# The up projection of a hybrid block as one sequence of 77 products, with weight splits three products ahead and the convolution in pieces

## The chip, the cores and the metric

The kernel runs on one core of a Trainium2 chip. The metric is the device time of one execution in microseconds (us), shown as the median of three runs. The core's engines are TensorE (PE in the profile; its weight loads PEld), VectorE (DVE), ScalarE (ACT), GpSimd (POOL) and SyncE (SP), and 16 DMA engines that all queues share. GpSimd and SP issue the transfers here: SP plain loads, GpSimd the transfers that add to their target.

## The reference

One transformer block on 512 tokens of width 1024: a recurrent mixer, a cross attention and a feed-forward network, each followed by a scaled residual and a layer norm. The change touches the feed-forward part:

```python
def conv_ffn(x, w_up, conv_w, conv_b, w_down):
    u = causal_dwconv(x @ w_up, conv_w, conv_b)
    gate, val = jnp.split(u, 2, axis=-1)
    return (jax.nn.gelu(gate) * val) @ w_down

x = layer_norm(ALPHA * x + ca, ln2_g[l], ln2_b[l])
ff = conv_ffn(x, ffn_w_up[l], ffn_conv_w[l], ffn_conv_b[l], ffn_w_down[l])
x = layer_norm(ALPHA * x + ff, ln3_g[l], ln3_b[l])
```

`w_up` is 1024 x 5632 in float32, the convolution has three taps along the tokens, `w_down` is 2816 x 1024.

## The kernel before

Every float32 product is made of three matmuls: each operand is split into a high part (cast to fp32r by ScalarE: `wh` for weights, line 125) and the rest (subtracted by VectorE: `wl`, line 126), and `mm3` (lines 155 to 157) adds high x high, and the two mixed terms. A split thus is a cast on ScalarE and then a subtraction on VectorE, for 128 x 1024 weights at a time; `wh` and `wl` have four buffers each.

The up projection saves work by Winograd's form of Strassen's scheme. Its weights lie in HBM as 11 column groups ("quads", q = 0 to 10), each of four blocks B11, B12, B21, B22 of 512 KB. Seven products replace eight. They are called here by the names that the changed kernel gives them, with the weights they use: M1 (B11), M2 (B21), M3 (B22), M7 (B22+B12), M6 (B11+B22+B12), M5 (T1 = B11+B12), M4 (B21+B11+B22+B12); M7.2 is that of quad 2. The left operands are sums of blocks of the activations (`xf` tiles, made by `forms_block`, lines 794 to 817, from four 128-token blocks after LN2: A11, A12 from blocks 0 and 1; S1 to S4 and A22 from blocks 2 and 3). One product is 24 matmuls of 256 columns. The sums of weights are made by transfers: `add` in `up_forms` (line 848) is a GpSimd transfer that adds HBM or SBUF data to an SBUF slot. In a quad the order is load B11, B21, B22; after the split of B22, B22 += B12; T1 = B11 loaded, += B12; B11 += the sum; B21 += that. Seven slots of 512 KB (`rawx` and the halves of the three `raw` tiles) hold the blocks in turn.

`quad` (line 870) writes, from quad 2 on, M3, M1, M2, M7, M6, M5, M4, with a split just ahead of each product, ScalarE's copies of partial results (line 880), VectorE's adds into `uu` (line 884), and then the whole convolution of the quad: for two halves and two `j`, ScalarE's first tap (`fc`, line 918), two taps on VectorE (line 920), GELU (line 922) and the product (line 923). For quads 0 and 1 M1 and M2 come first; M1.0 and M2.0 stand before the last transposes of the LN2 result (`x2_last`, line 927). The text sets no order here: the tile scheduler places the instructions on each engine by its own costs, and each engine then runs its list in order. The last slab ahead of this part multiplies by `ca_wo` (line 824); its block results go through `ln2_evict` (residual, statistics, norm; a small reciprocal-root op of each block runs on GpSimd, line 428). After it comes the down projection: `slab` over 22 `k` in units of two, each unit a split of `w_down` and of the hidden activations (`h_split`, line 939).

Of the kernel before, what the change touches and what calls it, by code (L numbers as in the profile page):

```python
# [40 lines left out]
def hybrid_block_kernel(  # L41
# [777 lines left out]
    def ln2_evict(b, ps):  # L819
        resid(b, ps, 512, 1024)  # L820
        norm(b)
        return lambda: forms_block(b)
# [16 lines left out]
    blocks = [q2.tile([P, 1024], F32, name="rawx")]  # L839
    for _ in range(3):  # L840
        r = wp.tile([P, 2048], F32, name="raw", tag="raw", bufs=3)
        blocks += [r[:, 0:1024], r[:, 1024:2048]]

    def up_forms(q, order):
        blk = lambda kh, ch: ffn_w_up[q, kh, ch]
        at = {n: blocks[(4 * q + i) % 7] for i, n in enumerate(order + ("T1",))}
        r1, r2, r3, r4 = (at[n] for n in ("B11", "B22", "B21", "T1"))
        load, add = nc.sync.dma_start, lambda d, s_: nc.gpsimd.dma_start(d, s_, accum_op=OP.add)
        src = {"B11": blk(0, 0), "B22": blk(1, 1), "B21": blk(1, 0)}
        for n in order:  # L850
            load(at[n], src[n])
        for n in order:
            yield split(at[n], (8, P), 16)
            if n == "B22":
                add(r2, blk(0, 1))
        load(r4, blk(0, 0))
        add(r4, blk(0, 1))
        add(r1, r2)
        add(r3, r1)
        for r in (r2, r1, r4, r3):  # L860
            yield split(r, (8, P), 16)
# [8 lines left out]
    def quad(q):  # L870

        early = q < 2
        us = up_forms(q, ("B11", "B21", "B22") if early else ("B22", "B11", "B21"))
        uu = (hf[3 + q] if early else raws[q % 2]).rearrange("p (c j t) -> p c j t", c=2, j=2)
        g2 = lambda t: t.rearrange("p (j t) -> p j t", j=2)
        t1, t2_ = slice(0, 256), slice(256, 512)

        def kept(bank, name):
            t = t2(name)
            A.copy(t, bank)  # L880
            return g2(t)

        def put(dst, bank, other):
            V.tensor_tensor(dst, g2(bank), other, op=OP.add)

        def third():
            b = mx_bank()
            product(b, "S4", next(us), True, True)
            return kept(b, "m3")

        if not early:
            m3 = third()
        bp = mm_bank()
        product(bp, "A11", next(us), True, False)
        m1 = kept(bp, "m1")
        b = mx_bank()
        product(b, "A12", next(us), True, True)
        put(uu[:, 0, :, t1], b, m1)
        if early:
            yield  # L900
            m3 = third()
        b4 = mm_bank()
        product(b4, "S3", next(us), True, False)
        m7 = kept(b4, "m7")
        product(bp, "S2", next(us), False, False)
        u2 = kept(bp, "u2")
        product(bp, "S1", next(us), False, True)
        put(uu[:, 1, :, t1], bp, m3)
        put(uu[:, 1, :, t2_], bp, m7)
        product(b4, "A22", next(us), False, True)  # L910
        put(uu[:, 0, :, t2_], b4, u2)
        for c in (1, 0):
            y = []
            for j in range(2):
                ft = j * NPAIR + 2 * q + c
                u, f = uu[:, c, j, :], t2("fc")
                w = lambda i: ncols[:, i * 44 + ft:i * 44 + ft + 1] if c else col(FCW + i * 44 + ft)
                A.activation(f, u, AF.Identity, bias=col(FCB + ft), scale=w(2))  # L918
                for d in (1, 2):
                    V.scalar_tensor_tensor(f[:, d:], u[:, :S - d], w(2 - d), f[:, d:], op0=OP.mult, op1=OP.add)  # L920
                y.append(f)
            A.activation(y[0], y[0], AF.Gelu_apprx_tanh)
            V.tensor_mul(hslice(2 * q + c), y[0], y[1])

    early = [quad(q) for q in range(2)]
    next(early[0])
    x2_last()
    next(early[1])
    for g in early:
        for _ in g:  # L930
# [72 lines left out]
```

## Time and profile before

| what | value |
|---|---|
| median of 3 runs | 874.77 us (873.73 to 875.7) |
| profiled execution, device time | 872.24 us |
| span of its profile | 870.5 us |
| PE busy | 806.2 us (93%) |
| DVE busy | 570.4 us (66%) |
| ACT busy | 376.3 us (43%) |
| DMA queue of the loads (q1), share of 16 engines | 33.4% |
| DMA queue of the adding transfers (q0) | 14.3% |

Times within the profile count from the span's start. "Idle before" in square brackets after an instruction is how long its engine stood before it, and what released it. The granted clock (PEclk) is that of TensorE, as a share of full speed. A matmul's own duration overlaps its neighbours', so a product's length is read from the starts of two neighbours.

### The profile page before, as it was taken

How to read it: one execution, taken by the hardware profiler on the slowest of the kernel's cores; microseconds unless marked ns; L12 is line 12 of the kernel's file. 1: busy time of each engine (PE TensorE's matmuls, PEld its weight loads, DVE VectorE, ACT ScalarE, POOL GpSimd, SP SyncE). 2: the span in 40 equal slices, each digit the busy share in tenths (PEclk: the TensorE clock that was granted, in tenths of full speed). 3: DMA queues.
4: the chain of work that ended last, by engine and by line, in shares of the span. 5: the costliest groups of instructions: out<-in, count | busy, mean ns of one | idle time of the engine just before them, and what ended most of it. 6: DMA issues, size and time to landing. Idle time of an engine off the chain costs nothing. (4 is left out here: it accounts for less than half of the span.)

```text
span 870.5 us, 11772 instructions
## 1 busy us (share of the span) xinstructions
PE 806.2 (93%) x4696; PEld 709.3 (81%) x4696; DVE 570.4 (66%) x944; ACT 376.3 (43%) x512; POOL 68.3 (8%) x96
## 2 busy tenths in 40 slices
PE   9979999999999999999995778888898788999996
PEld 7858877787798888889884778888898788888885
DVE  6463498898783893385596377776666768934227
ACT  2289543553252052273152355555544557721110
POOL 1000001001100000000000111101111110000001
PEclk9989999999999999999998788999989899999999
DMA  9936742353257142313401777677686866422202
GB/s 263 184 75 168 105 77 45 91 125 105 79 203 258 48 145 98 97 63 132 121 2 25 184 191 161 158 174 172 152 187 171 194 150 161 173 97 97 73 1 98
DMA packets 53183, 111.05 MB, mean 128 GB/s; under 512 B 3844, under 2 KB 21380, under 8 KB 53128
## 3 DMA queue, kind: packets, MB, share of 16 engines
q1 hardware_dynamic: 46208, 84.58, 33.4%
q0 software_dynamic: 6336, 23.07, 14.3%
q10 hardware_dynamic: 584, 2.64, 0.9%
q8 instruction: 37, 0.61, 0.3%
q14 instruction: 18, 0.15, 0.1%
HBM read 96.63 MB, written 2.12 MB: 113 GB/s over the span
## 5 line engine op out<-in xcount | busy, mean ns | idle before, releaser
L126 DVE TENSOR_TENSOR wl<-raw,wh 128x1024 fp32r<-128x1024 f32 x155 | 187.4, 1221 | 172.3 <-ACT wh L125 171.6
L125 ACT CAST wh<-raw 128x1024 fp32r<-128x1024 f32 x155 | 161.7, 1051 | 311.3 <-PE mm L157 126.2
L157 PE MATMUL mm<-xf,wl 128*128 128x256 f32 x440 | 133.0, 303 | 32.2 <-DVE wl L126 32.1
L155 PE MATMUL mm<-xf,wh 128*128 128x256 f32 x440 | 133.4, 304 | 8.9 <-ACT wh L125 8.1
L156 PE MATMUL mm<-xf,wh 128*128 128x256 f32 x440 | 131.0, 299 | 0.0
L157 PEld LDWEIGHTS mm<-xf,wl 128*128 128x128 f32 x440 | 93.0, 211 | 35.0 <-DVE wl L126 35.0
L155 PEld LDWEIGHTS mm<-xf,wh 128*128 128x128 f32 x440 | 93.1, 212 | 11.4 <-ACT wh L125 8.7
L156 PEld LDWEIGHTS mm<-xf,wh 128*128 128x128 f32 x440 | 92.9, 211 | 0.0
L156 PE MATMUL mm<-wl,hTh 128*128 128x512 f32 (+1 forms) x180 | 65.9, 366 | 0.0
L155 PE MATMUL mm<-wh,hTh 128*128 128x512 f32 (+1 forms) x180 | 65.8, 366 | 0.0
L157 PE MATMUL mm<-wh,hTl 128*128 128x512 f32 (+1 forms) x180 | 65.8, 365 | 0.0
L155 PE MATMUL mm<-wh,xTh 128*128 128x512 f32 x128 | 52.5, 410 | 0.4 <-DVE xTh L285 0.4
L156 PE MATMUL mm<-wl,xTh 128*128 128x512 f32 x128 | 52.0, 406 | 0.0
L157 PE MATMUL mm<-wh,xTl 128*128 128x512 f32 x128 | 51.5, 402 | 0.0
L155 PE MATMUL mm<-xTh,wh 128*128 128x512 f32 x128 | 51.2, 400 | 0.0
L157 PE MATMUL mx<-xf,wl 128*128 128x256 f32 x176 | 49.4, 280 | 1.9 <-DVE wl L126 1.9
L156 PE MATMUL mm<-xTl,wh 128*128 128x512 f32 x128 | 51.1, 399 | 0.0
L157 PE MATMUL mm<-xTh,wl 128*128 128x512 f32 x128 | 51.0, 398 | 0.0
L156 PE MATMUL mx<-xf,wh 128*128 128x256 f32 x176 | 49.5, 281 | 0.8 <-DVE xf L247 0.8
L155 PE MATMUL mx<-xf,wh 128*128 128x256 f32 x176 | 49.9, 284 | 0.2 <-ACT wh L125 0.2
L920 DVE SCALAR_TENSOR_TENSOR fc<-xfr,ncols,fc 128x511 f32<-128x511 f32 (+1 forms) x36 | 25.0, 748 | 24.1 <-ACT fc L918 24.1
L155 PEld LDWEIGHTS mm<-wh,hTh 128*128 128x128 f32 x180 | 34.0, 189 | 5.6
(312 smaller groups left out, 1764.0 us busy)
## 6 DMA issues: line engine op xcount, KB each, us to landing
raw<-in_ffn_w_up_dram SPq DMA_DIRECT2D x37, 512.0 KB, 4.5
raw<-in_w_in_dram SPq DMA_DIRECT2D x14, 1024.0 KB, 8.4
raw<-in_ffn_w_down_dram SPq DMA_DIRECT2D x10, 1024.0 KB, 5.1
raw<-in_ffn_w_up_dram POOLq DMA_DIRECT2D x19, 512.0 KB, 8.6
raw<-in_ca_wkv_dram SPq DMA_DIRECT2D x8, 1024.0 KB, 5.3
raw<-raw POOLq DMA_DIRECT2D x15, 512.0 KB, 4.7
raw<-in_w_out_dram SPq DMA_DIRECT2D x4, 1024.0 KB, 8.9
raw<-in_ca_wq_dram SPq DMA_DIRECT2D x4, 1024.0 KB, 5.0
```

What stands on the lines that cost most here:

```text
L125: A.copy(hv, src)
L126: V.tensor_sub(lv, src, f32(hv))
L155: T.matmul(ps, ah, bh, start=first, stop=False, skip_group_check=True)
L156: T.matmul(ps, ah, bl, start=False, stop=False, skip_group_check=True)
L157: T.matmul(ps, al, bh, start=False, stop=last, skip_group_check=True)
L920: V.scalar_tensor_tensor(f[:, d:], u[:, :S - d], w(2 - d), f[:, d:], op0=OP.mult, op1=OP.add)
```

## The change

The generator `quad` is replaced by `seq`, one list of 77 (product, quad) pairs, and `step(i)`, which writes for one product: the copies and adds that the product before left over (`posts`), the split of product i + 3, loads due then (`AHEAD`), the 24 matmuls, and one of five pieces of a finished quad's convolution. The list begins M1, M2 of quads 0, 1 and 2, goes on with a hand-made mix of quads 0 to 3, and from quad 3 on is M1, M2, M7, M6, M3 of the next quad, M5, M4. From step 6 on, the written order is kept on PE, ACT, DVE and GpSimd (`manual_schedule`); before that the scheduler places the instructions. There are nine slots (two halves of an `hf` tile are new), given out by `take` and `drop`. The first loads move into the `ca_wo` slab (`ffn_begin`), and quad 0 gets a second copy of B22, T3, to which B12 is added before M3.0. Splits for the first three units of the down projection are written in the last three steps.

```diff
-    def slab(xh, xl, w, c0, nk, evict, blocks=NB, late=0, mid=None, mid_k=4, halves=False, pre=None):
+    def slab(xh, xl, w, c0, nk, evict, blocks=NB, late=0, mid=None, mid_k=4, halves=False, units=None):
...
-    x2_last = slab(tok(oTh), tok(oTl), ca_wo[0], 512, KT, ln2_evict, late=4)
...
+    def ffn_begin():
+        half = lambda t: [t[:, 0:1024], t[:, 1024:2048]]
+        rt = [half(wp.tile([P, 2048], F32, name="raw", tag="raw", bufs=3)) for _ in range(3)]
+        slots[:] = rt[1] + rt[2] + [q2.tile([P, 1024], F32, name="rawx")] + rt[0] + half(hf[5])[::-1]
+        for q in range(3):
+            loads(q, ["B11", "B21"])
+        load(take(0, "T3"), blk(0, "B22"))
+        add(at(0, "T3"), blk(0, "B12"))
+        loads(0, ["B22"])
...
+    seq = [(n, q) for q in range(3) for n in ("M1", "M2")]
+    seq += [(n, int(q)) for n, q in (w.split(".") for w in
+            "M3.0 M7.0 M6.0 M3.1 M5.0 M4.0 M3.2 M7.1 M6.1 M3.3 M5.1 M4.1 M7.2 M6.2 M5.2 M4.2".split())]
+    for q in range(3, NQ):
+        seq += [(n, q) for n in ("M1", "M2", "M7", "M6")] + [("M3", q + 1)] * (q + 1 < NQ) + [("M5", q), ("M4", q)]
...
+    def split_of(i):
+        n, q = seq[i]
...
+        units[i] = split(at(q, src), (8, P), 16)
...
+        if n == "M3":
+            units[q, "summed"] = True
+            if t3 == "B22":
+                add(at(q, "B22"), blk(q, "B12"))
+            else:
+                drop(q, "B22")
+            if q not in (1, 2):
+                first_t(q)
+            if q < 3:
+                add(at(q, "B11"), at(q, t3))
+                add(at(q, "B21"), at(q, "B11"))
...
+    def step(i):
...
+        for f in posts:
+            f()
+        posts.clear()
+        if i + 3 < len(seq):
+            split_of(i + 3)
+        elif i + 3 - len(seq) < len(down_first):
+            down_first[i + 3 - len(seq)]()
+        for m, names in AHEAD.get(i, ()):
+            if names == "T1":
+                first_t(m)
+            else:
+                loads(m, names)
+        product(b, i, n in ("M1", "M2", "M3", "M7"), n in ("M2", "M3", "M4", "M5"))
+        if pieces:
+            pieces.pop(0)()
...
-    for q in range(2, NQ):
-        for _ in quad(q):
-            pass
...
+    slab(tok(oTh), tok(oTl), ca_wo[0], 512, KT, ln2_evict, late=4, mid=ffn_begin)
+    step(0)
+    forms_block(2)
+    step(1)
+    step(2)
+    forms_block(3)
+    for i in range(3, 6):
+        step(i)
+    ET = mybir.EngineType
+    with tc.manual_schedule(engines={ET.PE, ET.Activation, ET.DVE, ET.Pool}):
+        for i in range(6, len(seq)):
+            step(i)
+        for f in posts:
+            f()
```

Three places show how the instructions move. The first is TensorE at the transposes of block 3 (`xres3`, two groups into `mx` banks). Before, the groups stand side by side between M1.1 (`mm_3865`) and M2.1 (`mx_3899`):

```order
L157 MATMUL mm_3865<-xf_3532,wl_3870 128x256
L801 MATMUL mx_3840<-ident_89,xres3_2224 128x128 x4
L801 MATMUL mx_3845<-ident_89,xres3_2224 128x128 x4
L155 MATMUL mx_3899<-xf_3533,wh_3900 128x256
L156 MATMUL mx_3899<-xf_3533,wh_3900 128x256
```

In the change the second group stands two matmuls into M1.2 (`mm_3948`), and M2.1 comes after that product:

```order
L157 MATMUL mm_3857<-xf_3532,wl_3757 128x256
L799 MATMUL mx_3887<-ident_89,xres3_2224 128x128 x4
L155 MATMUL mm_3948<-xf_3532,wh_3829 128x256
L156 MATMUL mm_3948<-xf_3532,wh_3829 128x256
L799 MATMUL mx_3892<-ident_89,xres3_2224 128x128 x4
L157 MATMUL mm_3948<-xf_3532,wl_3830 128x256
```

The group that writes `mx_3892` has moved behind the start of a product. VectorE at the same place: before, the low part of A22 for block 2 (`xf_3538<-mx_3735`) stands ahead of the norm of block 3 (lines 670 to 679):

```order
L247 TENSOR_TENSOR xf_3537<-xfr_3540,xf_3537 128x4x128
L247 TENSOR_TENSOR xf_3538<-mx_3735,xf_3538 128x4x128
L670 BN_AGGR lnmv_3758<-st24_3528 128x2
L884 TENSOR_TENSOR hf_3769<-mx_3810,m1_3808 128x2x256
L427 TENSOR_SCALAR lnrs_3760<-lnmv_3758 128x1
L677 SCALAR_TENSOR_TENSOR xres3_2224<-xres3_2224,lnmv_3758,lngb_3461 128x512 x2
L679 SCALAR_TENSOR_TENSOR xres3_2224<-xres3_2224,lnrs_3760,lngb_3461 128x512 x2
```

In the change it is the last row here, and it reads the bank `mx_3806`:

```order
L675 SCALAR_TENSOR_TENSOR xres3_2224<-xres3_2224,lnmv_3763,lngb_3461 128x512 x2
L677 SCALAR_TENSOR_TENSOR xres3_2224<-xres3_2224,lnrs_3765,lngb_3461 128x512 x2
L810 SCALAR_TENSOR_TENSOR xfr_3540<-xfr_3540,xfr_3541 128x4x128
L126 TENSOR_TENSOR wl_3830<-rawx_3570,wh_3829 128x1024
L812 SCALAR_TENSOR_TENSOR xfr_3541<-xfr_3540,xfr_3541 128x4x128
L923 TENSOR_TENSOR hf_3545<-mx_3826,m1_3827 128x2x256
L126 TENSOR_TENSOR wl_3860<-raw_3567,wh_3859 128x1024
L245 TENSOR_TENSOR xf_3534<-xfr_3541,xf_3534 128x4x128
L245 TENSOR_TENSOR xf_3535<-xfr_3539,xf_3535 128x4x128
L245 TENSOR_TENSOR xf_3536<-xfr_3540,xf_3536 128x4x128
L245 TENSOR_TENSOR xf_3537<-xfr_3540,xf_3537 128x4x128
L245 TENSOR_TENSOR xf_3538<-mx_3806,xf_3538 128x4x128
```

The norm and more weight subtractions have moved ahead of it. The second place is GpSimd's queue for the first quads. Before, it holds the small op of block 3 and then B22, B11, B21 of quad 0 and the adds of quad 1:

```order
L428 TENSOR_TENSOR lnrs_3760<-lnrs_3760,neghalf_104 128x1
L848 DMA raw_3773<-in_ffn_w_up_dram 128x1024
L848 DMA rawx_3772<-raw_3773 128x1024
L848 DMA raw_3773<-rawx_3772 128x1024
L848 DMA raw_3775<-in_ffn_w_up_dram 128x1024
L848 DMA rawx_3772<-in_ffn_w_up_dram 128x1024
```

In the change the first row is the add into B21.0, then the small op of block 3, then B22.1, B11.1, B21.1, T1.1, B22.2, B11.2, B21.2, then two alike (B22.3 and T1.3) and T1.2:

```order
L843 DMA raw_3568<-raw_3568 128x1024
L426 TENSOR_TENSOR lnrs_3765<-lnrs_3765,neghalf_104 128x1
L843 DMA hf_3542<-in_ffn_w_up_dram 128x1024
L843 DMA raw_3569<-hf_3542 128x1024
L843 DMA raw_3569<-raw_3569 128x1024
L843 DMA hf_3542<-in_ffn_w_up_dram 128x1024
L843 DMA raw_3567<-in_ffn_w_up_dram 128x1024
L843 DMA rawx_3570<-raw_3567 128x1024
L843 DMA raw_3567<-rawx_3570 128x1024
L843 DMA raw_3568<-in_ffn_w_up_dram 128x1024 x2
L843 DMA hf_3542<-in_ffn_w_up_dram 128x1024
```

Quad 0's sums have moved ahead of block 3's small op, and the sums of quads 1 and 2 stand in one row. The third place is VectorE in the middle of the up projection. Before, the convolution of a quad stands in one piece, with a single subtraction among its taps:

```order
L920 SCALAR_TENSOR_TENSOR fc_4261<-hf_3770,ncols_275,fc_4261 128x511
L920 SCALAR_TENSOR_TENSOR fc_4265<-hf_3770,ncols_275,fc_4265 128x511
L920 SCALAR_TENSOR_TENSOR fc_4261<-hf_3770,ncols_275,fc_4261 128x510
L920 SCALAR_TENSOR_TENSOR fc_4265<-hf_3770,ncols_275,fc_4265 128x510
L920 SCALAR_TENSOR_TENSOR fc_4271<-hf_3770,cols_106,fc_4271 128x511
L923 TENSOR_TENSOR xfr_3541<-fc_4261,fc_4265 128x512
L920 SCALAR_TENSOR_TENSOR fc_4271<-hf_3770,cols_106,fc_4271 128x510
L920 SCALAR_TENSOR_TENSOR fc_4275<-hf_3770,cols_106,fc_4275 128x511
L126 TENSOR_TENSOR wl_4383<-raw_3773,wh_4382 128x1024
L920 SCALAR_TENSOR_TENSOR fc_4275<-hf_3770,cols_106,fc_4275 128x510
L884 TENSOR_TENSOR xfr_3539<-mx_4347,m1_4345 128x2x256
```

In the change a subtraction stands after every two taps:

```order
L126 TENSOR_TENSOR wl_5518<-raw_3567,wh_5517 128x1024
L936 SCALAR_TENSOR_TENSOR fc_5547<-xfr_3539,ncols_275,fc_5547 128x511
L936 SCALAR_TENSOR_TENSOR fc_5547<-xfr_3539,ncols_275,fc_5547 128x510
L126 TENSOR_TENSOR wl_5555<-raw_3569,wh_5554 128x1024
L936 SCALAR_TENSOR_TENSOR fc_5585<-xfr_3539,ncols_275,fc_5585 128x511
L936 SCALAR_TENSOR_TENSOR fc_5585<-xfr_3539,ncols_275,fc_5585 128x510
L923 TENSOR_TENSOR xfr_3540<-mx_5551,m1_5552 128x2x256
L126 TENSOR_TENSOR wl_5593<-raw_3568,wh_5592 128x1024
L939 TENSOR_TENSOR hf_3545<-fc_5547,fc_5585 128x512
L936 SCALAR_TENSOR_TENSOR fc_5621<-xfr_3539,cols_106,fc_5621 128x511
L936 SCALAR_TENSOR_TENSOR fc_5621<-xfr_3539,cols_106,fc_5621 128x510
L126 TENSOR_TENSOR wl_5628<-raw_3568,wh_5627 128x1024
```

The taps have moved apart, between the subtractions of the next quad.

## Rows read from the trace of the kernel before

**Rows 1.** The page's head.

```profile
span 870.5 us, 11772 instructions
```

**Rows 2.** Stretches: PE, PEld, DVE, ACT, POOL busy (instructions); PEclk, DMA share, GB/s.

```profile
500.00:720.00 220.00, 190.16 (x1484) 186.22 (x1483) 154.65 (x189) 117.59 (x153) 30.86 (x36) 0.91 0.73 171
...
742.50:800.00 57.50, 57.50 (x256) 47.61 (x255) 31.37 (x34) 21.12 (x23) 0.00 (x0) 1.00 0.37 128
...
632.00:636.60 4.60, 4.60 (x22) 4.60 (x23) 4.60 (x6) 1.05 (x1) 0.50 (x1) 0.50 0.77 200
...
560.00:570.00 10.00, 9.92 (x74) 9.72 (x74) 5.67 (x6) 4.53 (x6) 1.72 (x2) 0.86 0.90 227
```

**Rows 3.** TensorE in order of time, starts of M2.6, M7.6, its third matmul, M6.6.

```profile
624.71 0.28 PE L155 MATMUL mx<-xf,wh 128*128 128x256 f32 x1
...
627.43 0.28 PE L155 MATMUL mm<-xf,wh 128*128 128x256 f32 x1
...
631.83 0.58 PE L157 MATMUL mm<-xf,wl 128*128 128x256 f32 x1 [4.01 <-DVE wl L126]
...
636.69 0.41 PE L155 MATMUL mm<-xf,wh 128*128 128x256 f32 x1
```

**Rows 4.** Waits from 451 to 743 us: total, times, longest.

```profile
PE mm L157 <- DVE wl L126: 32.1, 12, 4.5
...
DVE fc L920 <- ACT fc L918: 27.2, 9, 4.4
```

**Rows 5.** VectorE in order of time around that stop: start, us, operation.

```profile
620.10 1.22 DVE L126 TENSOR_TENSOR wl<-raw,wh 128x1024 fp32r<-128x1024 f32 x1
625.27 2.78 DVE L920 SCALAR_TENSOR_TENSOR fc<-xfr,ncols,fc 128x511 f32<-128x511 f32 x4 [3.96 <-ACT fc L918]
...
630.56 1.22 DVE L126 TENSOR_TENSOR wl<-raw,wh 128x1024 fp32r<-128x1024 f32 x1
...
633.55 3.49 DVE L126 TENSOR_TENSOR wl<-raw,wh 128x1024 fp32r<-128x1024 f32 x3
...
644.82 1.29 DVE L884 TENSOR_TENSOR xfr<-mm,m 128x512 f32<-128x512 f32 x2 [2.39 <-PE mm L157]
```

**Rows 6.** ScalarE in order of time, the cast ahead of `fc`.

```profile
623.47 1.05 ACT L125 CAST wh<-raw 128x1024 fp32r<-128x1024 f32 x1 [4.27 <-DMA raw<-in_ffn_w_up_dram]
```

**Rows 7.** The tile `xf`: third matmuls, ns least/median/most, first and last start.

```profile
L157 PE MATMUL mm<-xf,wl x440: 276/276/582, 451.5 to 742.4; 128*128 128x256 f32 x147
```

**Rows 8.** TensorE at the start: transposes of block 3, and the start of M5.0.

```profile
463.02 1.64 PE L801 MATMUL mx<-ident,xres 128*128 128x128 f32 x8 [3.08 <-DVE xres L679]
...
491.26 0.58 PE L155 MATMUL mm<-xf,wh 128*128 128x256 f32 x1 [2.67 <-ACT wh L125]
```

**Rows 9.** VectorE at the start: norms of blocks 2 and 3, A22 between.

```profile
448.64 1.41 DVE L679 SCALAR_TENSOR_TENSOR xres<-xres,lnrs,lngb 128x512 f32<-128x512 f32 x2
...
459.44 0.68 DVE L247 TENSOR_TENSOR xf<-mx,xf 128x512 fp32r<-128x512 f32 x1
...
462.13 1.40 DVE L679 SCALAR_TENSOR_TENSOR xres<-xres,lnrs,lngb 128x512 f32<-128x512 f32 x2
```

**Rows 10.** DMA from 440 to 742 us: queues' packets, MB, share; issues, KB, us to landing.

```profile
q0 software_dynamic: 6192, 22.55, 40.2%
q1 hardware_dynamic: 7072, 22.87, 23.5%
...
raw<-in_ffn_w_up_dram POOLq DMA_DIRECT2D x18, 512.0 KB, 8.7
raw<-raw POOLq DMA_DIRECT2D x15, 512.0 KB, 4.7
```

**Rows 11.** The same from 472 to 479 us, one add after another.

```profile
q0 software_dynamic: 144, 0.52, 45.5%
...
raw<-in_ffn_w_up_dram POOLq DMA_DIRECT2D x1, 512.0 KB, 5.7
rawx<-raw POOLq DMA_DIRECT2D x1, 512.0 KB, 4.5
```

More of the change, by code (lines that the diff above doesn't have):

```diff
@@ L174, in run @@
                     mm3(pb, xh(k, b), xl(k, b), h[:, i, cs], l[:, i, cs], k == 0, k == nk - 1)
-        for u in slab_units(w, c0, nk):
+        for u in units or slab_units(w, c0, nk):
             k0, n, h, l = u
@@ L817, in forms_block @@
         put("A22", ps[1])
[L819 to L822, printed above, removed]
-    x2_last = slab(tok(oTh), tok(oTl), ca_wo[0], 512, KT, ln2_evict, late=4)
-    hf = [raws[2]] + [H8(F32, "hf") for j in range(5)]
+    h8 = [H8(F32, "hf") for j in range(5)]
+    hf = [raws[2]] + h8[1:] + h8[:1]
     def hslice(i):
         return hf[i // 4][:, (i % 4) * 512:(i % 4 + 1) * 512]
[L839 to L861, printed above, removed]
@@ L863, in product @@
-    def product(bank, n, u, first, last):
-        (h, l), (fh, fl) = u, forms[n]
+    slots, free = [], list(range(9))
+    def ffn_begin():
[7 more added lines that the diff above has]
+        loads(0, ["B22"])
@@ new lines, in hybrid_block_kernel, with take, drop, loads @@
+    held, units = {}, {}
+    def take(q, n):
+        ok = [f for f in free if not (q >= NQ - 2 and 5 <= f < 7) and not (q >= 7 and f == 8)]
+        held[q, n] = ok[0]
+        free.remove(ok[0])
+        return slots[ok[0]]
+    at = lambda q, n: slots[held[q, n]]
+    def drop(q, n):
+        free.append(held.pop((q, n)))
+    def loads(q, names):
+        for n in names:
+            load(take(q, n), blk(q, n if n != "T1" else "B11"))
+    def first_t(q):
+        loads(q, ["T1"])
+        add(at(q, "T1"), blk(q, "B12"))
@@ L865, in product @@
+    def product(bank, i, first, last):
+        (h, l), (fh, fl) = units.pop(i), forms[FORM[seq[i][0]]]
         for j in range(2):
@@ L868, in product @@
                     first and j == 0 and k == 0, last and j == 1 and k == 3)
[L870 to L930, printed above, removed]
-            pass
-    for q in range(2, NQ):
-        for _ in quad(q):
-            pass
+    banks, kept, uus, posts, pieces = {}, {}, {}, [], []
+    g2 = lambda t: t.rearrange("p (j t) -> p j t", j=2)
+    def keep(q, name, bank):
+        t = t2(name)
+        A.copy(t, bank)
+        kept[q, name] = g2(t)
+    def put(q, c, half, bank, name):
+        V.tensor_tensor(uus[q][:, c, :, half * 256:(half + 1) * 256], g2(bank), kept[q, name], op=OP.add)
@@ L937, in hybrid_block_kernel @@
+    where = {w: i for i, w in enumerate(seq)}
+    AHEAD = {}
+    for q in range(1, NQ):
+        if q > 2:
+            AHEAD.setdefault(max(where["M3", q] - 8, 1), []).append((q, ["B22"]))
+            AHEAD.setdefault(where["M1", q] - 7, []).append((q, ["B11", "B21"]))
+    for i, w in ((3, (1, ["B22"])), (6, (2, ["B22"])), (7, (1, "T1")), (12, (2, "T1"))):
+        AHEAD.setdefault(i, []).append(w)
     hTh, hTl = [], []
```

83 lines of the change are left out of this document (80 added, 3 removed).

## The prediction

> **What bounds the kernel now.** I read the stages first, then the up projection's own rows, then its waits. The tile's rows put the up projection between 451.2 and 742.5 us of the span (first and last third matmul at 451.5 and 742.4, with two before the one and its own 0.1 after the other) [rows 7]. It has 77 products of 24 matmuls. Where nothing is in the way, a product takes 2.72 us: two neighbours start at 624.71 and 627.43 [rows 3]. 77 times 2.72 is 209.4 us, so 291.3 - 209.4 = 81.9 us are lost. From 742.5 on TensorE has no gap, at clock 1.00 [rows 2], so what follows keeps its length of 128.0 us, and the change is worth what it takes out of the 81.9.
>
> The loss has two parts. **Once per quad**, TensorE stops in the product M7: its first two matmuls run and the third waits for `wl`, 4.01 us in the quad shown; the next product starts 9.26 us after M7 did [rows 3]. So 2.5 us beyond stop and product are gone: after the stop the granted clock is 0.50, the lower level, 1.2 GHz [rows 2]. Over the stage 12 such waits make 32.1 us [rows 4]. The cause is in VectorE's rows: between the subtraction at 620.10 and the next at 630.56 it idles 3.96 us for ScalarE's `fc`, then runs eight ops of the convolution, and only then makes the `wl` that TensorE needs [rows 5]. ScalarE's `fc` in turn stands behind a cast that waited 4.27 us for a transfer [rows 6]. A quad takes 24.9 us (1484 matmuls in 220 us, times 168), while the 16 DMA engines are busy 0.73 of the time, VectorE 0.70 and ScalarE 0.53 [rows 2]. Nothing is full: it is order and latency. **At the start**, up to about 500 us, TensorE waits for LN2 and then for one transfer after another [rows 8].
>
> **The change, part by part.** *Convolution in pieces.* VectorE keeps its 21 ops a quad: 7 subtractions at 3.49 / 3 = 1.16, 8 taps at 2.78 / 4 = 0.70, 6 adds and products at 1.29 / 2 = 0.65 [rows 5], sum 17.6 us against 19.04 us of TensorE for 7 products. ScalarE needs 0.53 x 24.9 = 13.3. In the new order no more than two taps and one product stand between two subtractions, about 2.0 us, and a subtraction is made three products, 8.2 us, before its use. The cast may start when the product before last has freed its buffer, at the start of the current one; copy, cast, and a lagging VectorE make it ready some 3 to 4 us in, so 4 us of slack are left in each step. The stop in M7 and its slow clock go, and I cost the pieces at nothing. If ScalarE and VectorE still wait for each other as now (27.2 us over 9 quads, 3.0 each [rows 4]), VectorE needs 20.6 a quad and becomes the bound; that is a rival below.
>
> *Transfers.* Each quad still has 4 loads by SP and 4 adds by GpSimd. In 302 us the adds took 40.2% and the loads 23.5% [rows 10]. An add is 144 packets [rows 11], so 6192 are 43 adds at 2.82 us of all 16 engines; a load is 71.0 / 22.87 MB x 0.524 = 1.63. A quad needs 4 x 2.82 + 4 x 1.63 = 17.8 us, 0.93 of 19.04. The trace has 0.90 over 10 us and 0.73 over the stage [rows 2], so this is the tightest resource once the stops go. The chain in a quad: the sum B22+B12 lands 8.7 us after issue, the next one into B11 4.7 later [rows 10]; with two issues of 0.9 that is 15.2 us, under 19.04, and the second result is wanted some 5 us after it lands. Nine slots instead of seven let loads run earlier. I take the engines at 0.84 from 470 us on, between 0.73 and 0.90 and nearer to the latter because loads can now fill the gaps between adds. Of 44 adds 4 and of 45 loads 9 are over by 470 (the 45th, for T3 of quad 0, is new: 1.63 us at most); left are 40 x 2.82 + 36 x 1.63 = 171.5, and 3 MB of the down projection at 3.1 a MB, together 181. 181 / 0.84 = 215 us: not before 685.
>
> *The start.* In the new order VectorE makes six subtractions and the norm of block 3 ahead of the A22 of block 2. That A22 ended at 460.1 before [rows 9]; ahead of it come three more subtractions (3.5), four norm passes with their statistics (3.2) and one add (0.65): 467.4. The second half of block 3's transposes writes the PSUM bank that this A22 reads (three banks, taken in turn), and it stands in TensorE's order in front of the rest of M1.2. TensorE has M1.0, M2.0, M1.1 and the first half done by about 461, so **a new stop of some 6 us** replaces the 3.08 us for LN2 [rows 8]. Then: the second half of the transposes 0.8 (half of 1.64 [rows 8]), the rest of M1.2 2.5 and slow clock 2.1, to 472.8; M2.1 and M2.2 to 478.2; M3.0, M7.0, M6.0 to 486.4 (the sums of quad 0 were made early). The tenth product starts there; before, the eighth waited until 491.26 [rows 8]. Also, block 3's small GpSimd op now queues behind the sum into B21.0, which waits for B11.0 (norm of block 2 done at 450.0 [rows 9], one subtraction 1.2, then 4.7 and 0.9: 456.8, wanted at about 457.4): nothing, up to 2 us if that add is late, hidden under the 467.4.
>
> Then **GpSimd's queue in written order**. The split of M3.1 cannot start before M2.2 has freed its buffers (478.2), ends at 480.5, and releases B22.1: landed 489.2; into B11.1: 493.9; issue of B21.1 (0.9), T1.1 (0.9), and B22.2 at 495.7: landed 504.4; B11.2: 509.1; behind it B21.2, B22.3 and T1.3 (0.9 each), then T1.2 at 511.8: landed 520.5. Its split ends 2.3 later, 522.8. TensorE stands at M5.2 by 516.7 (eleven products from 486.4, and 0.4 for T1.1, which lands at 503.5): **a second stop of 6.1 us**, with 2.5 of slow clock after it. M5.2 ends at 528.0; 56 products are left, 152.3 us at full pace: 680.3. The single-add rows at light load are 5.7 and 4.5 [rows 11]; with these T1.2 is there at 511 and the stop is gone. I take the loaded ones: three to four transfers are in flight.
>
> *Sum.* TensorE's pace gives 680.3, the transfers' share 685; both press at once, so I add 0.7 us a quad over the last eight: **686**. The up projection ends 56.5 us earlier. The profiled execution took 872.24 (span 870.5 [rows 1] and 1.74 around it): 815.7. The median shown is 2.5 above it: **818.3**. The splits of the first three `w_down` units ahead of time win nothing, since TensorE had no gap there; uncovered, one would cost 2.3.
>
> **A rule against the rows.** The rows have an add at 5.7 us alone and 8.7 in company [rows 10, 11]. The Trainium skill, "DMA: Bandwidth & Descriptors", section "Anatomy of one DMA — SWDGE (gpsimd) path", gives a transfer issued by GpSimd about 2.0 us plus bytes / 436e3, an estimate of 3.2 us for these 512 KB. By that the chain would be over long before TensorE needs it and the time would be that of the second case below. The trace disagrees (5.7), so its rows carry the sum.
>
> **The rivals.**
> - *Forecast, 0.50*: TensorE paces, with two stops at the start and a few us lost to transfers: 808 to 828.
> - *No stop at M5.2, full pace after, 0.18*: with 5.7 and 4.5 us the 57 products from 516.4 end at 671.4, 71.1 us earlier: 803.7. For it: adds alone are that fast [rows 11]. Against: they are not alone.
> - *The transfers bind, 0.18*: the share stays near the stage's 0.73 to 0.76, because the adds of a quad wait for one another. 470 + 181 / 0.76 = 708 gives 840; at 0.73, 850. For it: 0.73 is what the stage has; against: now VectorE and slots hold the transfers back.
> - *VectorE with its waits binds, 0.08*: 20.6 - 19.04 = 1.6 a quad, 12.5 over eight, on 680.3: 692.8, 825.
> - *Slower than before, 0.04*: one queue in written order makes the add chain the period. It decides when 8.7 + 4.7 + 1.8 grow to (742.5 - 528.0) / 8 = 26.8 us, 1.8 times. With both latencies doubled a quad is 28.6: 528.0 + 228.8 = 756.8, 889. Against: light and loaded SBUF adds differ by only 0.2 us [rows 10, 11].
> - *The stop only moves, 0.02*: some other wait of like size stands in each quad: within 0.2% of 874.8. The written order has no such lump on VectorE.
>
> **How the numbers follow.** The likeliest case gives 818. The range has the forecast, the second case down to 802, VectorE's case, and the half of the transfers' case up to 840: 0.50 + 0.16 + 0.08 + 0.09 = 0.83. A measurement of this kernel tells about 0.2% from no change. Faster by more: 0.50 + 0.18 + 0.18 + 0.08 = 0.94; within: 0.02; slower: 0.04.
>
> **What will show it.** Right: no wait of TensorE for `wl` over 1 us from 530 on, products 2.7 us apart, clock near 1.00, DMA share 0.82 to 0.92; a stop of about 6 us at the transposes of block 3, ended by VectorE's `xf` and not by `xres`; a stop before M5.2 ended by a cast that waited for T1's add; `w_down` starting near 686. Wrong: a period of 21 us or more with casts waiting for transfers (transfers bind); VectorE full with `fc` waits (handshake); no stop at M5.2; a new gap after the last product, which my sum has at zero.

## The result and the profile after

The changed kernel takes 838.86 us (median of 4 runs, 838.2 to 839.88), the kernel before 875.24 us beside it; the ratio is 0.9588, 95% interval 0.9571 to 0.9605. The forecast was 818, the range 802 to 840: the sign and the range held, but of the 56.5 us forecast 36.4 came. The study is about the 21 us between 818 and 839. (Between forecast and profile it is 24.8 us in the up projection, since the profile before was taken 2.5 us below its median and this one 1.0 above.)

The page of the changed kernel, answering to [rows 1]:

```profile
span 838.2 us, 11731 instructions
```

The up projection runs from 451.4 to 710.8 us; before, it ended at 742.5 [rows 7]. The rest behind it is 127.4 us, 128.0 forecast, so the whole difference lies in the up projection. TensorE's waits in it, for the changed kernel (engine, line <- releaser: us in all, times, longest):

```profile
PE mm L155 <- ACT u L919: 25.0, 6, 12.7
PE mm L155 <- ACT wh L125: 6.6, 1, 6.6
PE mx L155 <- DVE xf L245: 3.3, 1, 3.3
PE mx L799 <- ACT xfr L808: 0.8, 1, 0.8
```

The 32.1 us for `wl` [rows 4] are gone. In their place is a wait that does not stand among [rows 4]: for `u` at line 919, ScalarE's copy `u2` of bank P. That is the PSUM bank (the memory in which TensorE adds up its results) that M1, M6 and M5 of a quad share. M6 accumulates in bank P, the copy keeps that result for M4's output, and only then may M5 add to the same bank. TensorE's rows at the stops (start, length, instruction, idle before):

```profile
462.41 0.66 PE L799 MATMUL mx<-ident,xres 128*128 128x128 f32 x4 [0.82 <-ACT xfr L808]
474.71 0.36 PE L155 MATMUL mx<-xf,wh 128*128 128x256 f32 x1 [3.31 <-DVE xf L245]
509.52 0.58 PE L155 MATMUL mm<-xf,wh 128*128 128x256 f32 x1 [5.72 <-ACT u L919]
535.00 0.58 PE L155 MATMUL mm<-xf,wh 128*128 128x256 f32 x1 [12.72 <-ACT u L919]
616.24 0.39 PE L155 MATMUL mm<-xf,wh 128*128 128x256 f32 x1 [1.81 <-ACT u L919]
636.69 0.39 PE L155 MATMUL mm<-xf,wh 128*128 128x256 f32 x1 [1.13 <-ACT u L919]
678.38 0.39 PE L155 MATMUL mm<-xf,wh 128*128 128x256 f32 x1 [3.33 <-ACT u L919]
701.58 1.65 PE L155 MATMUL mm<-wh,hTh 128*128 128x512 f32 x3 [6.59 <-ACT wh L125]
```

They are the transposes of block 3, M3.0, M5.1, M5.2, M5.6, M5.7 and M5.9; the last row is three matmuls of the down projection that the scheduler put ahead of M5.10, which itself starts at 703.29, as its copy `u2` ends. The same by stretches (columns as in [rows 2]):

```profile
500.00:545.00 45.00, 26.56 (x196) 26.16 (x195) 25.93 (x33) 20.93 (x27) 6.07 (x7) 0.77 0.77 181
545.00:625.00 80.00, 77.91 (x685) 77.52 (x684) 69.67 (x85) 50.84 (x67) 13.04 (x15) 1.00 0.83 199
625.00:715.00 90.00, 78.90 (x643) 76.80 (x642) 74.09 (x89) 57.83 (x75) 11.31 (x13) 0.94 0.70 171
```

In the middle the forecast holds: TensorE nearly full, clock 1.00, DMA share 0.83 (0.73 before [rows 2]). The loss sits in two places, around 500 to 545 and behind 670. What stands ahead of the copy there is seen in ScalarE's rows, first at M5.2, then at M5.9:

```profile
528.27 1.04 ACT L125 CAST wh<-hf 128x1024 fp32r<-128x1024 f32 x1 [14.54 <-DMA hf<-in_ffn_w_up_dram]
...
533.84 0.63 ACT L934 ACTIVATE fc<-fc 128x512 f32<-128x512 f32 x1 [0.73 <-DVE fc L936]
534.38 0.57 ACT L919 COPY u<-mm 128x512 f32<-128x512 f32 x1
...
667.01 1.05 ACT L125 CAST wh<-raw 128x1024 fp32r<-128x1024 f32 x1 [7.30 <-DMA raw<-rawx]
...
677.23 0.63 ACT L934 ACTIVATE fc<-fc 128x512 f32<-128x512 f32 x1 [1.94 <-DVE fc L936]
677.76 0.57 ACT L919 COPY u<-mm 128x512 f32<-128x512 f32 x1
```

A cast waits for a sum made by transfers (T1.2, landed at 528.2; the sum in B11.9, landed at 666.9). Behind it ScalarE has to work off casts, first taps, copies and a GELU that waits for VectorE's taps, and the copy `u2` stands behind all of them. M5.2's own `wl` is ready at 530.6 (VectorE's row 529.35, 1.23 us), and TensorE still waits until 535.00: 8.3 us of that stop are the late transfer, 4.4 the queue behind it. M5.1 and M5.10 stop in the same way. The cast for M5.1 starts at 503.15 as T1.1 lands, its `wl` is ready at 505.47, and the copy ends at 509.46, with other casts, a table load of 1.28 us and the first GELU between. Ahead of M5.10, M4.10's cast waits until 697.4 for the sum in B21.10, and both the cast for the three early matmuls and the copy stand behind it.

### The profile page after: what moved, and what is told of

Its sections match the earlier page's. It is cut to its first block, busy times and chain, and to the rows that moved or that the text cites. A ratio compares the mean times of both kernels' runs of the same rounds, so it can differ in the third digit from the quotient of the medians.

```text
span 838.2 us, 11731 instructions
## 1 busy us (share of the span) xinstructions
PE 783.2 (93%) x4696; PEld 689.9 (82%) x4696; DVE 570.5 (68%) x944; ACT 374.7 (45%) x512; POOL 68.3 (8%) x96
## 5 line engine op out<-in xcount | busy, mean ns | idle before, releaser
L126 DVE TENSOR_TENSOR wl<-raw,wh 128x1024 fp32r<-128x1024 f32 x141 | 171.3, 1220 | 171.8 <-ACT wh L125 171.2
L125 ACT CAST wh<-raw 128x1024 fp32r<-128x1024 f32 x141 | 147.8, 1051 | 250.7 <-PE mm L157 122.4
L155 PE MATMUL mm<-xf,wh 128*128 128x256 f32 x440 | 125.4, 285 | 25.0 <-ACT u L919 25.0
L157 PE MATMUL mm<-xf,wl 128*128 128x256 f32 x440 | 124.4, 283 | 0.0
L156 PE MATMUL mm<-xf,wh 128*128 128x256 f32 x440 | 124.3, 283 | 0.0
L155 PEld LDWEIGHTS mm<-xf,wh 128*128 128x128 f32 x440 | 85.6, 194 | 27.0 <-ACT u L919 26.9
L157 PEld LDWEIGHTS mm<-xf,wl 128*128 128x128 f32 x440 | 85.3, 194 | 0.3 <-DVE wl L126 0.3
L156 PEld LDWEIGHTS mm<-xf,wh 128*128 128x128 f32 x440 | 85.5, 194 | 0.0
L426 POOL TENSOR_TENSOR lnrs<-lnrs,neghalf 128x1 f32<-128x1 f32 x12 | 11.1, 928 | 343.7 <-DVE lnrs L425 343.7
```

The source lines that it names most:

```text
L125: A.copy(hv, src)
L126: V.tensor_sub(lv, src, f32(hv))
L155: T.matmul(ps, ah, bh, start=first, stop=False, skip_group_check=True)
L156: T.matmul(ps, ah, bl, start=False, stop=False, skip_group_check=True)
L157: T.matmul(ps, al, bh, start=False, stop=last, skip_group_check=True)
L426: G.tensor_tensor(out_, out_, neghalf[:, 0:n], op=OP.pow)
```

## The experiments

All ratios are to the kernel before, run beside them; the changed kernel stands at 0.9588. In microseconds they are set against its 838.9. Single executions lie up to 0.8% from their median, and M5.1's stop alone was 5.72, 4.03 and 3.50 us in three kernels (the changed one, the one with the later load, the one with more descriptor memory) whose edits are not aimed at it, so differences under some 4 us are not read from times. The rows decide there.

**M5 in a bank of its own.**

```diff
-        if n in ("M2", "M3"):
+        if n in ("M2", "M3", "M5"):
             banks[q, n] = mx_bank()
-        b = banks[q, {"M1": "P", "M6": "P", "M5": "P", ...
+        b = banks[q, {"M1": "P", "M6": "P", ...
...
-            posts.append(lambda: (put(q, 1, 0, b, "m3"), put(q, 1, 1, b, "m7")))
+            posts.append(lambda: m5_out(q, b))   # bank + u2, then + m7 and + m3
```

> Edit: M5 accumulates in a PSUM bank of its own instead of adding onto bank P after M6; VectorE adds it to the copy u2 and then to m3 and m7 (one add more per quad, 0.65 us). TensorE then no longer waits for ScalarE's copy u2 before M5. Base: the changed kernel, 838.9 us. Theory (the shortfall against the forecast is that wait: ScalarE's queue in written order holds the copy behind casts that wait for transfers): the waits of M5.1, M5.2, M5.5 to M5.7, M5.9 and M5.10 (5.72, 12.72, 0.28, 1.81, 1.13, 3.33 and about 8.5 us) shrink to what M5's own split leaves (about 1.9 at M5.1, 8.3 at M5.2, 4.9 at M5.10, 0 elsewhere), 18 us less, and the time is 821 (818 to 829). Rival (the transfers are late as such, and the copy is only what happened to come last): TensorE stops for the next wl instead, at M4 or M1, by about as much: 836 to 840.

Measured: 830.35 us (826.18 to 833.35), ratio 0.949 (0.9449 to 0.9531), 8.5 us less. Two of TensorE's stops in this kernel:

```profile
526.29 0.58 PE L155 MATMUL mx<-xf,wh 128*128 128x256 f32 x1 [10.96 <-ACT wh L125]
...
665.90 0.58 PE L155 MATMUL mm<-xf,wh 128*128 128x256 f32 x1 [2.29 <-ACT m L919]
```

The waits for `u` are all gone, and the 5.72 at M5.1 with them. Two things remain: at M5.2 the wait for T1.2 itself (10.96; the 8.3 expected was too low), and a new one, 8.4 us in six places. Five are ahead of an M6, as the second row: M6 adds to bank P too and needs the copy `m1`, which stands behind M6's own cast, and that waits for the sum in B11. The sixth (3.03 us) is ahead of M4.10, which adds to M7's bank. So both theory and rival hold in part: the bank costs about 8.5 us, and late sums stop TensorE by another way where they are late.

**T1.2 written earlier.**

```diff
-    for i, w in ((3, (1, ["B22"])), (6, (2, ["B22"])), (7, (1, "T1")), (12, (2, "T1"))):
+    for i, w in ((3, (1, ["B22"])), (6, (2, ["B22"])), (7, (1, "T1")), (8, (2, "T1"))):
```

> Edit: load and add of T1.2 (B11 + B12 of quad 2) are written at step 8 instead of step 12, so that on GpSimd the add stands ahead of B22.2's instead of behind B22.3's and T1.3's. Base: the changed kernel, 838.9 us. Theory (M5.2's stop of 12.72 us is the place of one add in GpSimd's written order): the add lands by about 507 instead of 528.2, the cast that waited 14.54 us waits for nothing, and M5.2 stops for 0 to 3 us: 829 (826 to 833). Rival (the transfers of the first quads are one chain that is late as a whole): B22.2, B11.2 and B21.2 land some 5 to 8 us later for it, TensorE stops at M7.2, M6.2 or M4.2 instead: 836 to 841.

Measured: 829.78 us (828.28 to 831.41), ratio 0.9489 (0.9467 to 0.9511), 9.1 us less, as the theory had it. M5.1 and M5.2 in this kernel:

```profile
506.44 0.39 PE L155 MATMUL mm<-xf,wh 128*128 128x256 f32 x1 [3.85 <-ACT u L919]
524.30 0.58 PE L155 MATMUL mm<-xf,wh 128*128 128x256 f32 x1 [5.09 <-ACT u L919]
```

M5.2's stop falls from 12.72 to 5.09, not to 3: what is left is the copy again. Quad 2's other sums come a little later for it (the sum into B11.2 is issued at 508.07 against 506.68), not by the 5 to 8 us of the rival, and no stop at M7.2, M6.2 or M4.2 follows.

**Both together.** The two edits above in one kernel.

> Edit: both edits of before together, M5 in a bank of its own and T1.2 written at step 8. Base: the changed kernel, 838.9 us; alone they gave 830.4 and 829.8. Theory (two separate causes: a copy that stands behind casts on ScalarE, and one add in the wrong place on GpSimd): with T1.2 early the 10.96 us that M5.2 still waited for its own cast go, with the bank the 14.7 us for the copy that stayed with T1.2 early go in part: 8.5 + 9.1 less, 821 (815 to 825). Rival (the chain of adds as a whole sets the pace, and either edit alone already meets it): 828 to 831.

Measured: 824.85 us (823.86 to 825.01), ratio 0.9438 (0.9411 to 0.9465), 14.0 us less; alone 8.5 and 9.1, sum 17.6. So they overlap, and the theory holds at the upper end of its range (821, 815 to 825); M5.2 is the stop that both edits touch. Waits left in this kernel:

```profile
PE mm L155 <- ACT m L919: 8.5, 5, 3.6
PE mm L157 <- DVE wl L126: 3.7, 6, 1.2
```

No stop is longer than 3.6 us, and the longest are in quads 9 and 10.

**M4's split one step later.** If the copy stands behind M4's cast, writing that cast behind the copy must help.

```diff
+        if i + 2 < len(seq) and seq[i + 2][0] == "M4":
+            split_of(i + 2)
         if i + 3 < len(seq):
-            split_of(i + 3)
+            if seq[i + 3][0] != "M4":
+                split_of(i + 3)
```

> Edit: the split of M4 alone is written one step later (two products ahead), so that on ScalarE the copy u2 of bank P stands ahead of M4's cast, which waits for the sum in B21, instead of behind it; banks unchanged. Base: the changed kernel, 838.9 us. Theory (copy behind a cast that waits for a transfer): the waits in the steady quads (M5.6, M5.7, M5.9, M5.10) lose 5 to 9 us, those of M5.1 and M5.2 stay since there the cast of T1 is what waits: 831 (828 to 835). Rival (the casts' own lateness counts, and M4 stops instead): 837 to 842.

Measured: 838.37 us (836.16 to 843.14), ratio 0.9594 (0.9559 to 0.963): no change, the theory in this form falls. ScalarE at M5.9 in this kernel:

```profile
664.40 1.05 ACT L125 CAST wh<-raw 128x1024 fp32r<-128x1024 f32 x1 [6.99 <-PE mx L157]
...
674.61 0.63 ACT L934 ACTIVATE fc<-fc 128x512 f32<-128x512 f32 x1 [2.89 <-DVE fc L936]
675.15 0.57 ACT L919 COPY u<-mm 128x512 f32<-128x512 f32 x1
```

M4's cast no longer stands there, and the GELU ahead of the copy simply waits for VectorE longer, 2.89 instead of 1.94 us. The cast that starts it is M6's, written three steps before the copy (664.40 here, 667.01 above). The row names TensorE, which had long been done; GpSimd's next sum, at 664.95, waits for the landing of the sum in B11.9, and starts 0.55 us after the cast as it does in the changed kernel (667.56), where the row names that landing. Behind the cast ScalarE and VectorE hand first taps, taps and GELU to and fro, and the copy is at the end of that row.

**Twice the descriptor memory for GpSimd's transfers.**

```diff
-    nc = _bacc.Bacc(..., dynamic_dma_scratch_size=1024)
+    nc = _bacc.Bacc(..., dynamic_dma_scratch_size=2048)
...
-        return q2.tile([P, 512], dt, name=name, tag="t", bufs=9)
+        return q2.tile([P, 512], dt, name=name, tag="t", bufs=8)
```

> Edit: the descriptor memory of GpSimd's transfers is doubled, from 1024 to 2048 bytes per partition; eight instead of nine buffers of 2 KB for copies and taps make room for it. Base: the changed kernel, 838.9 us. Theory (GpSimd can have only three adds in flight for want of descriptor memory; T1.2's issue stood 4.14 us behind B21.2, B22.3 and T1.3 for that): the wait at T1.2's issue is gone, T1.2 lands some 4 us earlier, M5.2 stops some 4 us less: 835 (832 to 837). Rival (the 4.14 us are another wait, for the load of T1.2 or for its slot): the row stays as it was, 838 to 841. If the eight buffers matter, copies or taps of the steady quads wait, and the time goes up.

Measured: 836.53 us (835.69 to 840.42), ratio 0.9583 (0.9548 to 0.9618): no difference that can be told. GpSimd's rows from the sum into B21.2 on, of the changed kernel and then of this one (B21.2, the adds of B22.3 and T1.3, T1.2):

```profile
512.03 0.85 POOL L843 DMA_DIRECT2D raw<-rawx  x1 [4.49 <-DMA rawx<-raw]
512.68 1.99 POOL L843 DMA_DIRECT2D raw<-in_ffn_w_up_dram  x2
518.81 0.86 POOL L843 DMA_DIRECT2D hf<-in_ffn_w_up_dram  x1 [4.14 <-issue]
```

```profile
508.53 0.85 POOL L843 DMA_DIRECT2D raw<-rawx  x1 [5.01 <-DMA rawx<-raw]
509.13 2.01 POOL L843 DMA_DIRECT2D raw<-in_ffn_w_up_dram  x2
510.21 1.82 POOL L843 DMA_DIRECT2D hf<-in_ffn_w_up_dram  x1
```

The wait of 4.14 us is gone, so it was the descriptor memory: with 1024 bytes a fourth add waits until one of three has landed (B21.2 at 518.5, T1.2's issue 0.3 us later). But T1.2's cast starts at 524.26 here, 15.7 us after B21.2's issue; in the changed kernel it was 528.27, 16.2 us after. With four adds in flight T1.2's takes 14.0 us from issue to landing instead of 9.4, so it lands hardly sooner. What counts for T1.2 is its place in the row, as the experiment on that showed, not the limit.

**The first load of the down projection later.** A slot rule lets the down projection have two slots from quad 9 on; here from quad 10 on.

```diff
-        ok = [f for f in free if not (q >= NQ - 2 and 5 <= f < 7) and not (q >= 7 and f == 8)]
+        ok = [f for f in free if not (q >= NQ - 1 and 5 <= f < 7) and not (q >= 7 and f == 8)]
```

> Edit: quad 9 may use the two slots that the changed kernel gives up from there on, so that the first load of the down projection (1 MB, issued at 652.39 between loads of quads 9 and 10) has no buffer until quad 10 and is issued after quad 10's last load. Base: the changed kernel, 838.9 us. Theory (the sum into B11.9 took 8.4 us instead of 4.6 to 5.5 because that load and two others were in flight with it): the sum takes 5 to 7 us, M5.9's stop of 3.33 us goes to 1 or less, and part of the 8 us before M5.10 goes with quad 10's chain: 835 (832 to 837), if the down projection still gets its first weights in time. Rival (the stop of M5.9 has nothing to do with that load): 838 to 840, the sum as long as before.

Measured: 832.94 us (830.97 to 836.25), ratio 0.9553 (0.9511 to 0.9595). That interval overlaps the one of the changed kernel; the rows are plainer. The transfers during the sum into B11.9, of the changed kernel (658.5 to 667.5) and then of this one (656.7 to 662.5): the queue of the loads with its packets, MB and share of 16 engines, and the sum with its us to landing:

```profile
q1 hardware_dynamic: 601, 1.43, 40.8%
...
raw<-rawx POOLq DMA_DIRECT2D x1, 512.0 KB, 8.4
```

```profile
q1 hardware_dynamic: 142, 0.52, 22.0%
...
raw<-rawx POOLq DMA_DIRECT2D x1, 512.0 KB, 5.1
```

With fewer loads beside it the sum lands in 5.1 us instead of 8.4, and M5.9's stop of 3.33 us is gone. The wait of 6.59 ahead of M5.10 is 2.99. That one goes back to the sum into B21.10, which in the changed kernel ran beside the second load of the down projection, issued at 688.77, and here has no load beside it (689.2 to 697.4, then 684.5 to 689.7):

```profile
q1 hardware_dynamic: 693, 1.39, 59.4%
...
rawx<-hf POOLq DMA_DIRECT2D x1, 512.0 KB, 8.0
```

```profile
hf<-raw POOLq DMA_DIRECT2D x1, 512.0 KB, 5.0
```

So M5.9's stop, and about half of the one ahead of M5.10, come from loads of the down projection that run beside the last sums.

**No adding transfers.** Every block is used without its sums.

```diff
-    ..., add = nc.sync.dma_start, lambda d, s_: nc.gpsimd.dma_start(d, s_, accum_op=OP.add)
+    ..., add = nc.sync.dma_start, lambda d, s_: None
```

> Edit: no adding transfer at all; every block is loaded as before and used without its sums, so that M3 to M7 multiply other weights than they should. It bounds what all waits for sums cost, with the order of all engines kept. Base: the changed kernel, 838.9 us. Theory (every stop after the transposes goes back to a sum that lands late, by way of a cast, and of a copy behind the cast): 77 products of 2.72 from 451.4, with 1.4 for the transposes, 4.1 of waits for the sums of activations and some 2 us of lower clock, end at 668 instead of 710.8: 796 (792 to 802). Rival (ScalarE and VectorE in written order are a bound of their own): stops for copies and wl stay without any late transfer, 812 or more.

Measured: 801.4 us (799.96 to 807.67), ratio 0.9191 (0.9139 to 0.9242), 37.5 us less. Its waits and its middle:

```profile
PE mm L155 <- ACT u L919: 1.7, 2, 1.0
...
545.00:625.00 80.00, 80.00 (x708) 80.00 (x708) 74.22 (x89) 55.13 (x73) 0.00 (x0) 1.00 0.29 99
```

TensorE is full; ScalarE and VectorE in written order keep up with it, with nearly the same instructions. Their part in the stops is only to pass on, and to lengthen, what a late sum begins. The edit takes away the adds' latency and their share of the DMA engines together (0.29 is left of 0.83), so it does not tell these two apart. The 801 is also near the 803.7 of the case without a late transfer.

**Pieces, lead, and both undone.** First the convolution in one lump behind M4's last add, with the lead of three:

```diff
-            posts.append(lambda: (put(q, 0, 1, b, "u2"), pieces.extend(conv_pieces(q))))
+            posts.append(lambda: (put(q, 0, 1, b, "u2"), [f() for f in conv_pieces(q)]))
```

> Edit: the convolution of a quad is written at once behind M4's last add, as it stood before, and not in five pieces; sequence, lead of three and written order stay. Base: the changed kernel, 838.9 us. Theory (pieces are what removed the stop in M7: about 8 us of VectorE work in one lump and 3 us of handshake with ScalarE against 8.2 us of lead): stops of 2 to 4 us a quad come back on nine quads, 860 (850 to 870). Rival (the lead of three alone covers the lump): 839, within 3.

Then pieces with splits two products ahead, the loads one step later to fit, and two early units of the down projection instead of three:

```diff
-        if i + 3 < len(seq):
-            split_of(i + 3)
+        if i + 2 < len(seq):
+            split_of(i + 2)
```

> Edit: splits two products ahead instead of three, with the loads that are written by step moved one step later likewise; the first two units of the down projection instead of three. Base: the changed kernel, 838.9 us. Theory (the third product of lead is only partly needed: a split takes 3 to 4 us after its buffers are free, two products are 5.4 us, and casts that wait for sums then stand ahead of fewer copies): 842 (835 to 850). Rival (the lead is what carried the gain): a stop of 1.5 us or more in most products with taps beside them, 855 or more.

And the two together:

> Edit: the convolution in one lump and splits two products ahead, together. Base: the changed kernel, 838.9 us; alone they gave 847.7 and 844.2, with no stop over 0.8 us for wl behind the lump. Theory (either of the two covers the 8 us of VectorE work of a convolution, and only with both gone the stop of the kernel before comes back, 2 to 4 us with its lower clock in eight or nine quads): 862 (857 to 875). Rival (neither covers anything, the gain is in the sequence and the early start): 844 to 853, the sum of the two at most.

Measured: lump 847.74 us, ratio 0.969 (0.9653 to 0.9727); two ahead 844.15, ratio 0.9663 (0.9631 to 0.9695); both 870.37, ratio 0.9968 (0.9946 to 0.9989). So each by itself costs 5 to 9 us; the lump met neither its theory (850 to 870) nor its rival (839, within 3). M5.2's stop is 19.76 and 16.04 us in them, but TensorE comes to it earlier: counted from the first product, M5.2 starts 2.9 and 2.5 us later than in the changed kernel. Both together cost 31.5 of the 36.4 us; the other 4.9, which the sequence, the slots and the early loads brought on balance, were not taken apart. The stop of the kernel with both in one quad, and the end of it in the next:

```profile
650.04 0.39 PE L155 MATMUL mm<-xf,wh 128*128 128x256 f32 x1 [1.92 <-ACT wh L125]
651.76 0.58 PE L157 MATMUL mm<-xf,wl 128*128 128x256 f32 x1 [1.22 <-DVE wl L126]
...
676.58 0.58 PE L157 MATMUL mm<-xf,wl 128*128 128x256 f32 x1 [1.22 <-DVE wl L126]
```

The stop of about 3 us for one split stands in every quad again. Between the first GELUs of quads 4 and 7 a quad takes 24.9 us in the kernel before, 25.2 here, 21.3 with the lump alone, 20.8 with two ahead alone, 20.2 in the changed kernel and 19.04 without sums. The theory holds: either the pieces or the third product of lead covers the convolution's lump. The gain is one gain, and either part alone collects most of it.

**Without the written order.** From step 6 on the scheduler places the instructions again.

```diff
-    with tc.manual_schedule(engines={ET.PE, ET.Activation, ET.DVE, ET.Pool}):
-        for i in range(6, len(seq)):
-            step(i)
+    for i in range(6, len(seq)):
+        step(i)
```

> Edit: the written order is not kept; from step 6 on the scheduler places the instructions of all engines by its own costs, as it does in the kernel before. Sequence, lead and pieces stay. Base: the changed kernel, 838.9 us. Theory (sequence and lead carry the gain, and the written order costs some of it, where a copy or an add stands behind something late): 838, within 6. Rival (without the written order the scheduler draws splits together or pushes them behind the taps again): 850 or more.

Measured: 824.17 us (822.02 to 825.9), ratio 0.9449 (0.9403 to 0.9495): 14.7 us faster than the changed kernel, more than the theory gave it. Its waits, and its GpSimd row for T1.2:

```profile
PE mm L155 <- ACT u L919: 8.3, 7, 2.8
PE mm L155 <- ACT m L919: 6.0, 2, 4.0
...
500.26 0.88 POOL L843 DMA_DIRECT2D hf<-in_ffn_w_up_dram  x1 [2.62 <-issue]
```

T1.2 is issued at 500.26, not 518.81, and the waits for `u` are 8.3 us, not 25.0. The scheduler puts T1.2 early, as the second experiment did by hand; M5 still shares bank P. Which of its moves on ScalarE brings the rest was not taken apart.

**All four mended.** M5's bank, T1.2 at step 8, the descriptor memory, and the later load, with the written order kept.

> Edit: written order kept, with M5 in a bank of its own, T1.2 written at step 8, the descriptor memory of GpSimd's transfers doubled (eight buffers for copies and taps), and quad 9 allowed the two slots, so that the first load of the down projection comes later. Base: the changed kernel, 838.9 us. Theory (what lies between forecast and measurement is four things in separate places, a bank that waits for a copy, one add written late, three adds in flight, one load among the last sums): 14.0 for the first two together as measured, 5.9 for the load, 1 to 3 for the descriptor memory, 817 (813 to 822), TensorE's waits after 500 us under 6 us in all. Rival (they overlap, and the chain of sums sets the pace of the last quads anyway): 822 to 826.

Measured: 817.63 us (814.96 to 819.69, 6 runs), ratio 0.9351 (0.9323 to 0.9378), 21.2 us less than the changed kernel and the fastest of all that compute the whole block. Its waits, 440 to 745, those above 1.2 us:

```profile
PE mm L157 <- DVE wl L126: 3.8, 5, 1.8
PE mx L155 <- DVE xf L245: 3.5, 1, 3.5
PE mm L155 <- ACT m L919: 3.1, 4, 1.7
PE mm L156 <- DVE wl L126: 1.3, 1, 1.3
```

The expected 817 came, but the waits after 500 us are 10.3 us in all (3.8, 3.1, 1.3, 1.1 and 1.0), not under 6. What the descriptor memory gives in it was not measured apart. That it lands on the 818 of the forecast does not bear the forecast's sum out: it is another kernel, with other waits than the forecast has.

## Why the prediction was right in sign and wrong in size

The main step was right: the stop in M7 goes, and with it its lower clock. The time that TensorE loses beyond 77 products of 2.72 us was forecast at 25.2 us (686 less 451.4 and 209.4) and was 50.0. Term by term:

| place | forecast, us | measured, us |
|---|---|---|
| first nine products, with the transposes of block 3 and M3.0 | 486.4 - 451.2 - 24.5 = 10.7 | 484.6 - 451.4 - 24.5 = 8.7 |
| M5.1 | 0.4 | 5.9 + 1.7 = 7.6 |
| M5.2 | 6.1 + 2.5 = 8.6 | 12.9 + 2.5 = 15.4 |
| steady quads | 0.7 x 8 = 5.6 | 0.6 + 2.1 + 1.4 + 3.6 = 7.7 |
| ahead of M5.10 | 0 | 8.5 + 2.1 = 10.5 |

(A measured pair is the time between the end of the 2.72 us of one product and the start of the next, and what the next took beyond 2.72; for the steady quads, M5.5, M5.6, M5.7 and M5.9, the two are summed. 24.5 is nine times 2.72.) That the steady quads come near their forecast is luck: it meant delays by the transfers' share, and what was measured are four waits for `u2`.

- *The stop at the transposes* has the right kind of cause in the wrong place. VectorE finished the A22 of block 2 at 467.9, as forecast (467.4), but the second group of transposes did not wait for it. It started at 462.41, as ScalarE's copy out of the first group ended (461.78 + 0.58): the kernel's allocation gives both groups of block 3 one PSUM bank, and block 2's A22 reads another. "Three banks, taken in turn" was assumed and not read from anything. M3.0 writes that same bank, and there the stop came: 3.31 us, until VectorE's A22 of block 3, which reads the bank and is no operand of M3.0, ended at 474.6. So the tenth product started at 484.6, 1.8 us before the forecast. (M2.1 also did not come after M1.2, as the section on the change has it, but ran inside it, from 463.86.)
- *The chain of sums* was right to a microsecond at first (B11.1 landed at 493.4, 493.9 forecast), but by two errors that cancel: B22.1 took 6.9 us instead of 8.7, B11.1 6.6 instead of 4.7. B22.2 took 11.3 us instead of 8.7, beside B21.1 and T1.1, issued within 1.2 us of it, and T1.2's issue came at 518.81 instead of 511.8. The limit of three adds is in that row, but more descriptor memory did not land T1.2 sooner, since its add then took 14.0 us instead of 9.4.
- *The step that failed* is "4 us of slack are left in each step ... I cost the pieces at nothing". It counts only `wl`. It left out that M5 needs ScalarE's copy of M6's bank, in the same queue as casts and taps; one late sum there delays a product whose own weights are ready. The private bank took 8.5 us off, the earlier T1.2 9.1, both 14.0. Together with the later load and the descriptor memory it is 21.2 us.
- *The end* was costed at nothing: there is no new gap after the last product, as forecast, but one came just before it, at M5.10. The sums of quads 9 and 10 met loads of the down projection; with these later, the wait of 6.59 us was 2.99. What the early splits of `w_down` are worth was not tried.
- *Transfers bind* (840) met the number by another way. The share was 0.83 in the middle, where TensorE was nearly full, and 0.77 and 0.70 in the stretches that hold the two losses. The run without adds shows that nearly all the stops behind the transposes start from sums. The mean share over a stage does not tell when one sum lands: where transfers met, single adds were late (11.3 us for B22.2, 8.4 for B11.9), and these set the stops. That the measured time still lies in the range, 1.1 us from its end, is owed to this case, and is luck.
- *The rule on the adding transfer*: the estimate of 3.2 us from the Trainium skill ("DMA: Bandwidth & Descriptors", section "Anatomy of one DMA — SWDGE (gpsimd) path") is too short here as well; single sums take 4.5 us at best and 8.4 beside loads.

## What to carry to other kernels

When a stop is costed away, follow every operand of each product through the engines' queues, the bank that it adds to as well as its weights: here a copy that frees a bank stood behind a cast that waited for a transfer. Splitting up a lump and starting its consumers earlier are two covers for the same lump, so their gains do not add. An order that is kept as written also keeps its mistakes: as first written it was 14.7 us slower than the scheduler's own order, and with four places mended 6.5 us faster (the mends were not tried under the scheduler).

## What the runs showed of the hardware that was not expected

With `dynamic_dma_scratch_size=1024` a fourth adding transfer of 512 KB waits at its issue (4.14 us); with 2048 it does not. But the fourth then takes 14.0 us from issue to landing instead of 9.4, and lands 15.7 us after the first's issue, as against 16.2. A sum from SBUF to SBUF lands in 5.1 us beside loads that take 22.0% of the engines and in 8.4 us where they take 40.8%; another in 5.0 us with no load beside it and in 8.0 us where loads take 59.4%.
